# Plain MLP products of chunks 0 and 1 beside attention, Strassen blocks for chunks 2 and 3 only, split weights kept in DRAM

## The chip, the cores and the metric

The kernel runs on one core of one Trainium2 chip. The metric is the device time of one execution in microseconds. The kernel before takes 2695.92 us, the median of three runs (2693.48 to 2704.14). The profile is of one further execution of 2692.31 us, whose span in the trace is 2690.6 us.

## The reference

One layer over 2048 tokens of width 1024, all in float32:

```
h = rmsnorm(x);  q, k, v, u, vg = split(h @ w_in)                 # w_in 1024 x 2560
a = stick_breaking_attention(q, k, v)                             # 8 heads of 64, causal:
    # A[t,s] = sigmoid(z_ts) * prod_{s<j<t} (1 - sigmoid(z_tj)),  z = q.k / 8
b = gelu(u) * (W_s layernorm(gelu(vg)) + b_s)                     # 8 groups, 128x128 each
x = x + concat(rmsnorm(a), rmsnorm(b)) @ w_out                    # 1024 x 1024
x = x + square(relu(rmsnorm(x) @ w_up)) @ w_down                  # 1024 x 4096, 4096 x 1024
out = rmsnorm(x)
```

## The kernel before

The 2048 tokens are four chunks of 512. Every float32 product is made of three: each operand is split into a high part (a copy rounded by ScalarE, ACT, L79, or L82 with a gain) and a low part (the difference, VectorE, DVE, L80 or L83), and `mm3` (L85 to L89) issues high by high (L87), high by low (L88) and low by high (L89), each 128 x 128 against 128 x 512, into one PSUM tile. These are "products" below. A "set" is one operand tile of 4 x 128 x 512 with its two halves.

The stages in order:

- `proj` multiplies with w_in: chunks 0 and 1 in one pass, then chunk 2, then chunk 3. `weight` (L112) loads 512 KB tiles into `st` (3 buffers) and splits each into `w_in` (5 buffers), in each of the three passes: 20 tiles a pass.
- `attention` (L282 to L377) is a generator of short steps, 320 of them over the four chunks. One step issues two products for z (L311, L312, on the diagonal a mask L314 too), two sigmoids on ACT (L317, L319), a scan and a multiplication on DVE (L322 or L325, L323 or L326), then for an earlier step four transposes (L336) with the split of `aT` (L79 on ACT, L80 on DVE), and for one still earlier two products with v (L354, L355). L364 writes a head's output.
- `Out(c)` (L417 to L531) is the output projection of a chunk: `operands` transposes and splits, `weights` (L462) loads and splits w_out, `product` makes 192 products and adds to x (L489), `turn` norms and transposes into the MLP's right operand, kept in SBUF for chunks 0 and 1 and stored to `h_d` for 2 and 3.
- `up_plain` (L550 to L568) makes the first MLP product of chunks 0 and 1 plainly: 16 turns of 96 products. `keep_acts` (L542) forms four Strassen sums on GpSimd (POOL, L536 to L539) and stores seven matrices to `s_d` from POOL's queue (L544).
- `down_seven` (L663 to L780) makes the second product of two chunks by Strassen's seven block products: 8 groups of 168, 1344 in all. `sums_of_h` forms the sums of `h_d` on POOL, stored to `th_d`; `right_operands` (L585) loads and splits seven sets of them; `up_seven` (L595) does the first product of chunks 2 and 3 in seven blocks, 1344 products, and `down_seven` the second.

What orders the work: each engine runs its instructions in the order in which the Tile scheduler put them, and the DMAs that SP issues (`nc.sync`) start in SP's order, those of `nc.gpsimd` in POOL's. Pools of tiles decide when a buffer is free. `together(main, side, ratio)` (L784) takes one part of `main` up to its next yield and then `ratio` steps of `side`: attention is `side`, with R_A = 1.0 beside `proj`, R_O = 1.0 beside `Out` 0 and 1, R_U = 0.87 beside `up_plain`, which yields every 6 products. When attention has ended, these follow alone (L860 to L870): `Out` 2 and 3, `down_seven(0)` with `sums_of_h`, `right_operands`, `up_seven(1)`, `down_seven(1)`.

Of the kernel before, what the change touches and what calls it, by code (L numbers as in the profile page):

```python
# [8 lines left out]
F32 = mybir.dt.float32  # L9
# [7 lines left out]
P = 128  # L17
# [17 lines left out]
def block_kernel(ctx: ExitStack, tc: tile.TileContext, x, x_t, gmix, w_in, ln_g, ln_b, sgw, sgb,  # L35
# [30 lines left out]
    b_d = dram.tile([T, SBW], F32, name="b_d")  # L66

# [39 lines left out]
    def proj(cs, places, sp, gated_first):  # L107
# [170 lines left out]
    R_A, R_O, R_U = 1.0, 1.0, 0.87  # L278
# [107 lines left out]
    h_d = dram.tile([4, P, 2, 2, TC], F32, name="h_d")  # L386
    th_d = [dram.tile([P, 4, TC], F32, name=f"th_d{i}") for i in range(4)]
    s_d = [[dram.tile([7, P, 4, TC], F32, name=f"s_d{p}_{g}") for g in range(NG)] for p in range(2)]

    class Room:  # L390


        def __init__(self, pool, psum, bufs, big=None):
            self.pool, self.psum, self.bufs, self.big_pool = pool, psum, bufs, big or pool

        def big(self, shape, dtype=F32):
            return self.big_pool.tile([P] + list(shape), dtype, name="big", bufs=self.bufs["big"])

        def get(self, name, shape, dtype=F32):
            return self.pool.tile([P] + list(shape), dtype, name=name, bufs=self.bufs[name])  # L400

# [3 lines left out]
        def raw8(self, shape):  # L405
            return self.get("raw8", shape)

# [8 lines left out]

    class Out:  # L417


        def __init__(self, c, room, place):  # L420
            self.c, self.rm, self.place = c, room, place

        def operands(self):
            rm, c = self.rm, self.c
            bm = self.bm = rm.big([2, 4, TC], F32R)
            self.rbs = []
            for t2 in range(2):
# [492 lines left out]
```

## Time and profile before

| | |
|---|---|
| median of three runs | 2695.92 us |
| profiled execution; its span | 2692.31 us; 2690.6 us |
| PE busy; weight loads (PEld) | 2422.6 us (90%); 1955.5 us (73%) |
| DVE, ACT, POOL busy | 1936.3 us (72%); 1271.6 us (47%); 616.3 us (23%) |
| mean granted clock of TensorE | 0.955 |
| DMA queues of SP and of POOL, share of 16 engines' span | 44.7%; 2.9% |

By the trace's names the stages lie so: `proj` of chunks 0 and 1 from 0 to 265 us, of 2 and 3 with attention to 620, `Out` 0 and 1 with attention to 815, `up_plain` with attention to 1457 and alone to 1490, `Out` 2 and 3 to 1666, `down_seven(0)` to 2013, `right_operands` to 2042, `up_seven(1)` to 2350, `down_seven(1)` to the end. Matmuls are pipelined and their recorded lengths overlap, so PE's busy time is more than its work; how densely products follow each other is read from their number in a stretch. The clock is given as a share of full speed (1.0 is 2.4 GHz, 0.5 is 1.2 GHz).

### The profile page before, as it was taken

The page shows a single profiled execution, that of the slowest core. Times are in us where ns is not written, and L with a number is a line of the kernel's source. Part 1 is how long each engine was busy: PE and PEld are TensorE (multiplying, and loading weights), DVE is VectorE, ACT ScalarE, POOL GpSimd, SP SyncE. Part 2 cuts the span into 40 slices and gives each one's busy share as a digit, 9 for nine tenths or more (in the row PEclk, how much of TensorE's full clock was granted, in tenths as well). Part 3 has the DMA queues.
Part 4 walks back from the last instruction along what each step waited for, and adds up shares of the span by engine and source line. Part 5 has one row for each costly group of instructions (what it writes and reads, how often), then busy time and mean ns, then how long its engine had stood idle before and what let it go on. Part 6 is the DMA issues. An engine that isn't in the chain of part 4 may idle for free.

```text
span 2690.6 us, 30409 instructions
## 1 busy us (share of the span) xinstructions
PE 2422.6 (90%) x11136; PEld 1955.5 (73%) x11136; DVE 1936.3 (72%) x2424; ACT 1271.6 (47%) x2144; POOL 616.3 (23%) x395
## 2 busy tenths in 40 slices
PE   7999989898898989999999594799986999989997
PEld 5887777776677777777777483578875888778886
DVE  6634788878888878888894453577786666567777
ACT  6314556455646656665664432233344454433333
POOL 3100021101101121212122202543223232133331
PEclk9999999999999999999999797899997999999999
DMA  6347755457544454444441627554235444554422
GB/s 203 102 125 229 195 167 164 146 153 215 164 121 143 140 149 125 141 125 145 125 146 69 240 86 297 189 186 157 102 138 181 162 145 156 214 218 161 157 102 94
DMA packets 159941, 422.48 MB, mean 157 GB/s; under 512 B 12720, under 2 KB 29104, under 8 KB 151088
## 3 DMA queue, kind: packets, MB, share of 16 engines
q1 hardware_dynamic: 148064, 389.08, 44.7%
q0 software_dynamic: 7424, 29.36, 2.9%
q10 hardware_dynamic: 4304, 2.10, 0.3%
q8 instruction: 88, 1.44, 0.2%
q14 instruction: 61, 0.50, 0.1%
HBM read 303.05 MB, written 117.44 MB: 156 GB/s over the span
## 4 chain that ended last, share of the span: by engine, by line
PE 60%; DVE 20%; DMA 8%; ACT 4%; issue 4%; POOL 3%; SPq 1%; POOLq 0%; DVEq 0%; ACTq 0%
PE mm L88 17%; PE mm L89 17%; PE mm L87 17%; DVE w L80 4%; DVE pr L325 4%; PE tr L336 3%; DVE b L326 2%; PE av L354 2%; DVE aT L80 1%; PE av L355 1%; PE z L311 1%; PE z L312 1%; DMA raw<-h_d 1%; DMA raw<-s_d 1%; DVE pr L322 1%
## 5 line engine op out<-in xcount | busy, mean ns | idle before, releaser
L87 PE MATMUL mm<-big,w 128*128 128x512 f32 x960 | 380.0, 396 | 30.5 <-ACT w L79 29.6
L87 PE MATMUL mm<-w,w 128*128 128x512 f32 x896 | 349.7, 397 | 56.5 <-ACT w L79 56.5
L88 PE MATMUL mm<-big,w 128*128 128x512 f32 x960 | 378.8, 395 | 0.0
L89 PE MATMUL mm<-big,w 128*128 128x512 f32 x960 | 378.7, 394 | 0.1
L88 PE MATMUL mm<-w,w 128*128 128x512 f32 x896 | 359.5, 401 | 18.3 <-DVE w L80 16.5
L89 PE MATMUL mm<-w,w 128*128 128x512 f32 x896 | 355.9, 397 | 0.0
L80 DVE TENSOR_TENSOR w<-raw,w 128x1024 fp32r<-128x1024 f32 (+1 forms) x192 | 247.9, 1292 | 65.6 <-ACT w L79 65.0
L325 DVE TENSOR_TENSOR_SCAN pr<-kk,pr,zeros 128x513 f32<-128x513 f32 x192 | 259.8, 1353 | 40.1 <-ACT kk L317 37.0
L317 ACT ACTIVATE kk<-z 128x512 f32<-128x512 f32 (+2 forms) x320 | 171.0, 534 | 242.1 <-PE z L312 141.1
L79 ACT ACTIVATE w<-raw 128x1024 fp32r<-128x1024 f32 (+1 forms) x192 | 165.7, 871 | 185.7 <-PE mm L89 98.3
L336 PE MATMUL tr<-ident,b 128*128 128x128 f32 x1088 | 191.3, 284 | 61.5 <-DVE b L326 38.7
L79 ACT ACTIVATE w<-big 128x1024 fp32r<-128x1024 f32 x96 | 101.6, 1059 | 296.5 <-PE mm L89 199.6
L87 PEld LDWEIGHTS mm<-w,w 128*128 128x128 f32 x896 | 170.5, 192 | 97.0 <-ACT w L79 61.6
L87 PEld LDWEIGHTS mm<-big,w 128*128 128x128 f32 x960 | 182.5, 190 | 69.4 <-ACT w L79 30.2
L88 PEld LDWEIGHTS mm<-w,w 128*128 128x128 f32 x896 | 172.9, 193 | 63.8 <-DVE w L80 27.8
L80 DVE TENSOR_TENSOR w<-big,w 128x1024 fp32r<-128x1024 f32 x96 | 134.8, 1404 | 116.7 <-ACT w L79 116.7
L336 PEld LDWEIGHTS tr<-ident,b 128*128 128x128 f32 x1088 | 134.6, 145 | 105.9 <-DVE b L326 46.0
L89 PEld LDWEIGHTS mm<-big,w 128*128 128x128 f32 x960 | 182.3, 190 | 40.0 <-DVE w L80 0.8
L88 PEld LDWEIGHTS mm<-big,w 128*128 128x128 f32 x960 | 182.9, 190 | 37.4
L79 ACT ACTIVATE aT<-tr 128x512 fp32r<-128x512 f32 (+1 forms) x320 | 172.9, 542 | 67.3 <-PE tr L336 66.0
L80 DVE TENSOR_TENSOR aT<-tr,aT 128x512 fp32r<-128x512 f32 (+1 forms) x320 | 190.7, 596 | 13.8 <-ACT aT L79 13.5
L89 PEld LDWEIGHTS mm<-w,w 128*128 128x128 f32 x896 | 173.2, 193 | 36.0
(188 smaller groups left out, 5107.7 us busy)
## 6 DMA issues: line engine op xcount, KB each, us to landing
raw<-s_d SPq DMA_DIRECT2D x56, 1024.0 KB, 4.8
kt<-k_d SPq DMA_DIRECT2D x160, 256.0 KB, 4.7
big<-in_w_down SPq DMA_DIRECT2D x16, 2048.0 KB, 10.1
st<-in_w_in SPq DMA_DIRECT2D x60, 512.0 KB, 5.1
s_d<-acts POOLq DMA_DIRECT2D x16, 1792.0 KB, 7.7
s_d<-acts SPq DMA_DIRECT2D x16, 1792.0 KB, 6.2
vt<-v_d SPq DMA_DIRECT2D x80, 256.0 KB, 2.7
t<-in_w_out SPq DMA_DIRECT2D x32, 512.0 KB, 6.2
```

The source lines that it names most:

```text
L79: nc.scalar.activation(hi, src, AF.Copy)
L80: nc.vector.tensor_tensor(lo, src, hi.bitcast(F32), ALU.subtract)
L87: nc.tensor.matmul(ps, lh, rh, start=first, stop=False, skip_group_check=more)
L88: nc.tensor.matmul(ps, lh, rl, start=False, stop=False, skip_group_check=more)
L89: nc.tensor.matmul(ps, ll, rh, start=False, stop=last, skip_group_check=more)
L311: nc.tensor.matmul(z[:, :Z], ql, kt[:, 0, :Z], start=True, stop=False)
L312: nc.tensor.matmul(z[:, :Z], ql, kt[:, 1, :Z], start=False, stop=not diag)
L317: nc.scalar.activation(kk[:, :L], z[:, :L], AF.Sigmoid, scale=-QK_SCALE)
L325: nc.vector.tensor_tensor_scan(pr[:, ::-1], kk[:, ::-1], zeros, carry[tb], ALU.mult, ALU.add)
L326: nc.vector.tensor_tensor(b, b, pr[:, 1:TC + 1], ALU.mult)
L336: nc.tensor.transpose(tr[:, tb * P:(tb + 1) * P], bs[tb][:, j * P:(j + 1) * P], ident)
L354: nc.tensor.matmul(av[:, t0:], vt[:, j, :], aT[:, 0, t0:], start=first, stop=False)
```

## The change

- `weight` splits w_in once, in the pass of chunks 0 and 1, and stores each split tile (1 MB) to `wi_d` from POOL's queue (L123 of the changed kernel). The passes of chunks 2 and 3 load 1 MB from there straight into `w_in` on SP (L118), with no split.
- `Out(0)` stores its split w_out to `wo_d`, the other chunks load it. `product` yields every 6 products instead of 12, `turn` twice as often, and R_O is 0.5.
- One pool of 14 tiles of 8 KB a partition ("t8") holds all operands, inputs and sums of the stages beside attention, in turn.
- `up_plain` forms no Strassen sums and stores the activations themselves to `act_d` from SP; R_U is 0.49. `down_plain` replaces `down_seven(0)`: 8 groups of 192 products, 1536 instead of 1344.
- The order is now `up_plain`, `Out(2)` and `down_plain` beside attention; then, with attention done, `Out(3)` woven with the middle of `down_plain`, then the rest of `down_plain`, then alone `right_operands`, `up_seven`, `down_seven`.
- `right_operands` loads four sets from `h_d` and forms the differences on DVE between the splits; `sums_of_h` and `th_d` are gone. The gains of the norms are loaded once.

The diff, cut (what it removes stands in the functions above; the rest of `Out` changes only tiles and their shapes):

```diff
         def weight(col, k2):
+
+            w = sp.tile([P, 2, 2, 512], F32R, name="w_in", bufs=5)
+            if cs[0] > 0:
+                nc.sync.dma_start(w.bitcast(F32), wi_d[col, k2])
+                return w
             st = sp.tile([P, 2, 512], F32, name="st", bufs=3)
             nc.sync.dma_start(st, w_in[col, :, 2 * k2:2 * k2 + 2, :])
-            w = sp.tile([P, 2, 2, 512], F32R, name="w_in", bufs=5)
             split(w[:, 0], w[:, 1], st)
+            nc.gpsimd.dma_start(wi_d[col, k2], w.bitcast(F32))
             return w
 
...
 
-    R_A, R_O, R_U = 1.0, 1.0, 0.87
+    R_A, R_O, R_U = 1.0, 0.5, 0.49
+
...
     y_d = [dram.tile([P, NTB, D], F32, name=f"y_d{c}") for c in range(NC)]
-    h_d = dram.tile([4, P, 2, 2, TC], F32, name="h_d")
-    th_d = [dram.tile([P, 4, TC], F32, name=f"th_d{i}") for i in range(4)]
-    s_d = [[dram.tile([7, P, 4, TC], F32, name=f"s_d{p}_{g}") for g in range(NG)] for p in range(2)]
+    h_d = [[dram.tile([P, 4, TC], F32, name=f"h_d{i}_{kk}") for kk in range(2)] for i in range(2)]
+    act_d = [dram.tile([P, DFF // P, TC], F32, name=f"act_d{i}") for i in range(2)]
+    s_d = [dram.tile([7, P, 4, TC], F32, name=f"s_d{g}") for g in range(NG)]
...
+            return self.t8(shape, F32R), self.t8(shape, F32R)
+
...
+    def split4(hl, src):
+        for j in range(0, 4, 2):
+            split(hl[0][:, j:j + 2, :], hl[1][:, j:j + 2, :], src[:, j:j + 2, :])
+
...
+            if self.c > 0:
+                for i in range(2):
+                    nc.sync.dma_start(w[i].bitcast(F32), wo_d[half, part, i])
...
                     ts_ = slice(tb * P, (tb + 1) * P)
                     ps = rm.ps()
                     for e in range(4):
-                        mm3(ps, m[:, 0, e, ts_], m[:, 1, e, ts_], ws[e][0], ws[e][1], e == 0, e == 3)
+                        mm3(ps, m[0][:, e, ts_], m[1][:, e, ts_], ws[0][:, e, :], ws[1][:, e, :], e == 0, e == 3)
+                        if e == 1:
+                            yield
                     nc.vector.scalar_tensor_tensor(ys[tb][:, hs], ps, rr[tb], ys[tb][:, hs], ALU.mult, ALU.add)
...
+                    for i in range(2):
+                        nc.sync.dma_start(wo_d[half, part, i], ws[i].bitcast(F32))
 
             yield from group(0, 1, self.bm, self.rbs)
...
+    def keep_acts(q, acts):
+
+        a11, a12, a21, a22, s1, s2, s4 = (acts[:, i] for i in (0, 1, 6, 3, 4, 5, 2))
+        nc.vector.tensor_tensor(s1, a21, a22, ALU.add)
+        nc.vector.tensor_tensor(s2, s1, a11, ALU.subtract)
+        nc.vector.tensor_tensor(a21, a11, a21, ALU.subtract)
+        nc.vector.tensor_tensor(s4, a12, s2, ALU.subtract)
+        nc.sync.dma_start(s_d[q // 4][:, :, q % 4, :].rearrange("i p t -> p i t"), acts)
...
 
         for q in range(16):
-            acts = rm.get("acts", [7, TC])
+            acts = rm.t8([2, 2, TC])
+            st = rm.t8([2, 8, P])
...
+                            k == 0, k == KD - 1)
                         if k % 2 == 1 and k < KD - 1:
                             yield
...
+            for i in range(2):
+                nc.sync.dma_start(act_d[i][:, 2 * q:2 * q + 2, :], acts[:, i])
...
+            return a
+
+        def right(n, g):
+            st = rm.t8([4, 512])
+            nc.sync.dma_start(st, w_down[4 * g * P:4 * (g + 1) * P, n * 512:(n + 1) * 512]
+                              .rearrange("(f p) d -> p f d", p=P))
+            b = rm.pair([4, 512])
+            split4(b, st)
+            return b
+
+        ND = 8
+        c_now, n_now = 0, 0
+        for g in range(ND):
+            lefts, rights = {}, {}
+            for turn in range(4):
+                if turn == 2:
+                    c_now = 1 - c_now
+                elif turn > 0:
+                    n_now = 1 - n_now
+                c, n = c_now, n_now
+                if c not in lefts:
...
+                for tb in range(NTB):
+                    ts_ = slice(tb * P, (tb + 1) * P)
+                    ps = rm.ps()
+                    for k in range(4):
+                        mm3(ps, a[0][:, k, ts_], a[1][:, k, ts_], b[0][:, k, :], b[1][:, k, :], k == 0, k == 3)
+                        if k == 1:
+                            yield
+                    y = ys[4 * c + tb]
+                    nc.vector.tensor_tensor(y[:, ns], ps, y[:, ns], ALU.add)
+                    if g == ND - 1 and turn % 2 == 1:
+                        finish(rm, rm.t4([D], BF16), c, tb, y)
+                    yield
+
...
-        for i in ORDER:
-            st = rm.raw8([4, TC])
-            src = th_d[i - 3] if i >= 3 else h_d[:, :, (0, 1, 1)[i], (0, 0, 1)[i], :].rearrange("j p t -> p j t")
-            nc.sync.dma_start(st, src)
-            hc[i] = rm.big([2, 4, TC], F32R)
+        b = {}
+        for i, kk, name in ((0, 0, "raw8"), (1, 0, "raw8"), (1, 1, "acts"), (0, 1, "acts")):
...
+        def minus(dst, x, y):
             for j in range(0, 4, 2):
-                split(hc[i][:, 0, j:j + 2, :], hc[i][:, 1, j:j + 2, :], st[:, j:j + 2, :])
-            yield
...
+        def keep(i, src):
+            t = rm.big([2, 4, TC], F32R)
+            hc[i] = t
+            split4((t[:, 0], t[:, 1]), src)
+
+        keep(0, b11)
+        minus(b11, b12, b11)
+        keep(4, b11)
+        minus(b11, b22, b11)
+        keep(5, b11)
+        minus(b12, b22, b12)
+        keep(6, b12)
+        keep(1, b21)
+        minus(b21, b21, b11)
+        keep(3, b21)
+        keep(2, b22)
...
+        together(o.operands(), side, R_U)
+        together(o.product(), side, R_U)
+        together(o.turn(), side, R_U)
+        down = down_plain(rm)
+        assert together(down, side, R_U) is OPEN
+    with tc.tile_pool(name="ext", bufs=1, side="right", reuse_waits="tile") as ext, \
+            tc.tile_pool(name="ps_x2", bufs=5, space=PSUM, reuse_waits="tile") as ps_x2:
+        rm3 = Room(ext, ps_x2, dict(t8=8, t4=1))
+        o = Out(3, rm3)
+        for part in (o.operands, o.product, o.turn):
+            together(part(), down, 0.8)
+        together(down)
+    low.close()
     mm_stack.close()
-    with tc.tile_pool(name="ps_b", bufs=8, space=PSUM, reuse_waits="tile") as ps_b:
-        with tc.tile_pool(name="op2", bufs=1, reuse_waits="tile") as op2:
-            rm = Room(op2, ps_b, dict(big=4, w8=4, t4=10, ys=8, raw8=4))
-            o2, o3 = Out(2, rm, 0), Out(3, rm, 1)
-            together(o2.operands())
-            together(o3.operands())
-            together(o2.product())
-            turn = o2.turn()
-            together(o3.product(), turn, 0.25)
-            together(turn)
-            together(o3.turn())
-        with tc.tile_pool(name="mlp", bufs=1, reuse_waits="tile") as mlp:
-            rm = Room(mlp, ps_b, dict(big=7, w8=5, raw8=2, acts=2, t2=4))
-            main = down_seven(0, rm)
-            for _ in range(8):
-                next(main)
-            together(main, sums_of_h(rm), 0.25)
-            together(main)
-            hc = [None] * 7
-            together(right_operands(rm, hc))
-            together(up_seven(1, hc, rm))
-            together(down_seven(1, rm))
+    with tc.tile_pool(name="ps_b", bufs=8, space=PSUM, reuse_waits="tile") as ps_b, \
+            tc.tile_pool(name="mlp", bufs=1, reuse_waits="tile") as mlp:
+        rm = Room(mlp, ps_b, dict(big=7, w8=5, raw8=2, acts=2, t2=3))
+        hc = [None] * 7
+        right_operands(rm, hc)
+        together(up_seven(hc, rm))
+        together(down_seven(rm))
```

Two or three places show how the instructions move (names are the program's; in the changed kernel lines differ: L89 to L91 are the three products, L320 and L321 z, L345 the transposes, L363 and L364 av, L638 the sum into y, L82 the low part of a split).

PE beside attention in `up_plain`, in the kernel before. `mm` is a product of `up_plain`, z, tr and av are one step of attention:

```order
L336 MATMUL tr<-ident,b 128x128 x4
L354 MATMUL av<-aT,vt 128x512
L355 MATMUL av<-aT,vt 128x512
L87 MATMUL mm<-big,w_10410 128x512
L88 MATMUL mm<-big,w_10410 128x512
L89 MATMUL mm<-big,w_10410 128x512
L87 MATMUL mm<-big,w_10410 128x512
L88 MATMUL mm<-big,w_10410 128x512
L89 MATMUL mm<-big,w_10410 128x512
L311 MATMUL z<-kt,qt 128x256
L312 MATMUL z<-kt,qt 128x256
```

Here 6 products stand between two steps. In the changed kernel, at the same part of `up_plain`:

```order
L363 MATMUL av<-aT,vt 128x512
L364 MATMUL av<-aT,vt 128x512
L89 MATMUL mm<-t_6782,t_9205 128x512
L90 MATMUL mm<-t_6783,t_9205 128x512
L91 MATMUL mm<-t_6782,t_9206 128x512
L89 MATMUL mm<-t_6782,t_9205 128x512
L90 MATMUL mm<-t_6783,t_9205 128x512
L91 MATMUL mm<-t_6782,t_9206 128x512
...
L91 MATMUL mm<-t_5908,t_9488 128x512
L320 MATMUL z<-kt,qt 128x384
L321 MATMUL z<-kt,qt 128x384
```

What moved: the same step is now followed by 12 products, so the attention that stood beside `up_plain` alone reaches into `Out(2)` and `down_plain`.

DVE in the later part of the changed kernel's `down_plain`, with attention and `Out(3)` done. `t_12276` and `t_12278` are the sums y of one chunk, `t_12280` and `t_12282` those of the other, `mm` the product's PSUM tile, L82 the low part of a set for a later turn (`t_15341`, `t_15349`), in two pieces:

```order
L638 TENSOR_TENSOR t_12280<-mm,t_12280 128x512 x2
L638 TENSOR_TENSOR t_12282<-mm,t_12282 128x512
L82 TENSOR_TENSOR t_15341<-t_15338,t_15340 128x1024
L638 TENSOR_TENSOR t_12282<-mm,t_12282 128x512
L82 TENSOR_TENSOR t_15341<-t_15338,t_15340 128x1024
L638 TENSOR_TENSOR t_12276<-mm,t_12276 128x512 x2
L638 TENSOR_TENSOR t_12278<-mm,t_12278 128x512
L82 TENSOR_TENSOR t_15349<-t_15346,t_15348 128x1024
L638 TENSOR_TENSOR t_12278<-mm,t_12278 128x512
L82 TENSOR_TENSOR t_15349<-t_15346,t_15348 128x1024
L638 TENSOR_TENSOR t_12276<-mm,t_12276 128x512 x2
L638 TENSOR_TENSOR t_12278<-mm,t_12278 128x512
```

What moved: in place of the additions and Strassen forms of `down_seven(0)` there is one addition of 128x512 for each 12 products and eight pieces of split for each 192. A set is split in the turn before the one that uses it, and its second piece stands behind that turn's last addition.

SP at the end of the MLP of chunks 0 and 1, in the kernel before. `big` holds the finished outputs, `raw` are the tiles of `right_operands`, the last row the first weights of `up_seven`:

```order
L690 DMA out_y<-big 128x1024 x3
L589 DMA raw_16259<-th_d_92 128x2048
L690 DMA out_y<-big 128x1024
L589 DMA raw_16266<-th_d_93 128x2048
L690 DMA out_y<-big 128x1024 x4
L589 DMA raw_16273<-h_d 128x4x512
L589 DMA raw_16280<-th_d_90 128x2048
L589 DMA raw_16287<-h_d 128x4x512
L598 DMA raw_16294<-in_w_up 128x2x1024
```

And in the changed kernel (L648 stores the outputs, L654 loads `h_d`, L681 the weights of `up_seven`):

```order
L648 DMA out_y<-t_12276 128x1024 x2
L648 DMA out_y<-t_12278 128x1024 x2
L654 DMA raw_15932<-h_d_0_91 128x2048
L654 DMA raw_15934<-h_d_0_93 128x2048
L654 DMA acts<-h_d_1_94 128x2048
L654 DMA acts<-h_d_1_92 128x2048
L681 DMA raw_15983<-in_w_up 128x2x1024
```

What moved: the loads of the right operands stood among the output stores and stand behind all eight of them now; four 1 MB sets are loaded instead of seven.

## Rows read from the trace of the kernel before

**Rows 1.** The page: busy time by engine; PE by fortieths of the span, in tenths.

```profile
PE 2422.6 (90%) x11136; PEld 1955.5 (73%) x11136; DVE 1936.3 (72%) x2424; ACT 1271.6 (47%) x2144; POOL 616.3 (23%) x395
PE   7999989898898989999999594799986999989997
```

**Rows 2.** Windows by stage: length, busy PE, PEld, DVE, ACT, POOL (instructions), clock, DMA, GB/s.

```profile
265.00:620.00 355.00, 324.92 (x1618) 261.54 (x1618) 291.59 (x448) 197.04 (x386) 42.63 (x41) 0.98 0.58 167
...
1490.00:1666.00 176.00, 107.59 (x489) 87.99 (x489) 72.32 (x103) 57.47 (x100) 25.60 (x27) 0.80 0.58 216
1666.00:2013.00 347.00, 323.58 (x1344) 260.14 (x1344) 264.26 (x250) 119.14 (x125) 135.06 (x52) 0.95 0.43 156
2013.00:2042.00 29.00, 0.64 (x2) 0.44 (x2) 19.20 (x21) 13.62 (x17) 4.83 (x5) 0.59 0.70 254
...
815.00:2042.00 1227.00, 1059.42 (x4938) 854.58 (x4938) 899.85 (x1017) 582.41 (x1005) 304.57 (x174) 0.94 0.46 153
0.00:50.00 50.00, 40.57 (x156) 30.52 (x157) 31.04 (x52) 32.90 (x51) 13.41 (x24) 0.97 0.74 242
```

**Rows 3.** Windows: attention beside `proj`, beside `up_plain`, and `up_seven` alone.

```profile
500.00:600.00 100.00, 96.36 (x490) 78.68 (x489) 79.32 (x115) 53.48 (x101) 4.09 (x3) 1.00 0.55 156
2060.00:2340.00 280.00, 280.00 (x1237) 231.82 (x1236) 171.71 (x234) 142.37 (x235) 78.42 (x57) 1.00 0.43 155
1050.00:1150.00 100.00, 93.00 (x472) 74.86 (x471) 84.74 (x103) 61.55 (x121) 20.08 (x12) 1.00 0.47 144
```

**Rows 4.** PE's waits: line waited for, us in total, times, longest.

```profile
PE mm L87 <- ACT w L79: 86.1, 11, 33.0
PE tr L336 <- DVE b L326: 38.7, 23, 4.8
```

**Rows 5.** The chain that ended last, at 1640 us and in the norms at 2007: start, us, what.

```profile
1639.73 24.17 DMA raw<-s_d
...
2007.28 1.40 POOL nf_r L73
2008.71 1.28 DVE big L689
```

**Rows 6.** ACT by line: a split's high part; steps of attention from 815 us on.

```profile
L79 ACT ACTIVATE big<-raw 128x1024 fp32r<-128x1024 f32 x14 | 14.1, 1048 | 15.0 <-DMA raw<-h_d 8.4 <-issue 4.6 <-DMA raw<-th_d 1.9
L317 ACT ACTIVATE kk<-z x194: 262/597/648, 815.1 to 1436.2; 128x512 f32<-128x512 f32 x155, 128x128 f32<-128x128 f32 x13, 128x256 f32<-128x256 f32 x13, 128x384 f32<-128x384 f32 x13
```

**Rows 7.** PE's timeline around one full step beside `up_plain`: start, us, engine, line.

```profile
1202.66 0.40 PE L89 MATMUL mm<-big,w 128*128 128x512 f32 x1
1202.89 0.39 PE L311 MATMUL z<-kt,qt 128*128 128x512 f32 x1
...
1204.26 0.39 PE L87 MATMUL mm<-big,w 128*128 128x512 f32 x1
```

**Rows 8.** DVE by line and form: busy us, mean ns, idle before.

```profile
L325 DVE TENSOR_TENSOR_SCAN pr<-kk,pr,zeros 128x513 f32<-128x513 f32 x192 | 259.8, 1353 | 40.1 <-ACT kk L317 37.0
...
L80 DVE TENSOR_TENSOR aT<-tr,aT 128x512 fp32r<-128x512 f32 x224 | 152.0, 679 | 13.8 <-ACT aT L79 13.5
L326 DVE TENSOR_TENSOR b<-b,pr 128x512 f32<-128x512 f32 x192 | 148.7, 775 | 12.0
L678 DVE TENSOR_TENSOR big<-mm,big 128x512 f32<-128x512 f32 x208 | 139.6, 688 | 18.4 <-PE mm L89 18.4
...
L80 DVE TENSOR_TENSOR w_in<-st,w_in 128x1024 fp32r<-128x1024 f32 x60 | 74.8, 1253 | 17.3 <-ACT w_in L79 16.7
...
L80 DVE TENSOR_TENSOR big<-raw,big 128x1024 fp32r<-128x1024 f32 x14 | 16.6, 1218 | 8.1 <-ACT big L79 8.1
```

**Rows 9.** DMA issues: KB each, median us from issue to landing.

```profile
raw<-s_d SPq DMA_DIRECT2D x56, 1024.0 KB, 4.8
...
s_d<-acts POOLq DMA_DIRECT2D x16, 1792.0 KB, 7.7
s_d<-acts SPq DMA_DIRECT2D x16, 1792.0 KB, 6.2
```

More of the change, by code (lines that the diff above doesn't have):

```diff
@@ L66, in block_kernel @@
     b_d = dram.tile([T, SBW], F32, name="b_d")
+    wi_d = dram.tile([5, KD // 2, P, 2, 2, 512], F32, name="wi_d")
+    wo_d = dram.tile([2, 2, 2, P, 4, 512], F32, name="wo_d")
     def rsqrt_mean(pool, ssq, n, count, tag):
@@ L473, in weights @@
-            return ws
+            rm = self.rm
+            w = rm.pair([4, 512])
+            if self.c > 0:
+                for i in range(2):
+                    nc.sync.dma_start(w[i].bitcast(F32), wo_d[half, part, i])
+                return w
+            st = rm.t8([4, 512])
+            nc.sync.dma_start(st, w_out[part * 512:(part + 1) * 512, half * 512:(half + 1) * 512]
+                              .rearrange("(n p) d -> p n d", p=P))
+            for n in range(4):
+                split(w[0][:, n], w[1][:, n], st[:, n], outg_t[:, part * 4 + n:part * 4 + n + 1])
@@ L839, in block_kernel @@
         base.close()
-        with tc.tile_pool(name="hp", bufs=1, reuse_waits="tile") as hp:
-            hTs = []
-            with tc.tile_pool(name="op", bufs=1, reuse_waits="tile") as op:
-                rm = Room(op, ps_mm, dict(big=4, w8=3, t4=5, ys=5), hp)
-                for c in range(2):
-                    while steps[0] < 16 * (c + 1) * (c + 2) + NTB + LAG:
-                        next(side)
-                    o = Out(c, rm, None)
-                    together(o.operands(), side, R_O)
-                    together(o.product(), side, R_O)
-                    together(o.turn(), side, R_O)
-                    hTs.append(o.hT)
-            with tc.tile_pool(name="upp", bufs=1, reuse_waits="tile") as upp:
-                rm = Room(upp, ps_mm, dict(big=4, w8=4, t4=2, acts=2), hp)
-                main = up_plain(0, hTs, rm)
-                if together(main, side, R_U) is OPEN:
-                    together(main)
-                for _ in side:
-                    pass
@@ new lines, in block_kernel @@
+        gfin_t = gains.tile([P, D], F32, name="gfin_t")
+        low = ExitStack()
+        mp = low.enter_context(tc.tile_pool(name="mp", bufs=1, reuse_waits="tile"))
+        gmlp_t = mp.tile([P, D], F32, name="gmlp_t")
+        nc.sync.dma_start(gmlp_t, gmlp.broadcast_to([P, D]))
+        nc.sync.dma_start(gfin_t, gfin.broadcast_to([P, D]))
+        rm = Room(mp, ps_mm, dict(t8=N8, t4=2))
+        hTs = []
+        for c in range(2):
+            while steps[0] < 16 * (c + 1) * (c + 2) + NTB + LAG:
+                next(side)
+            o = Out(c, rm)
+            together(o.operands(), side, R_O)
+            together(o.product(), side, R_O)
+            together(o.turn(), side, R_O)
+            hTs.append(o.hT)
@@ new lines, in block_kernel @@
+        together(up_plain(hTs, rm), side, R_U)
+        while steps[0] < 16 * 3 * 4 + NTB + LAG:
+            next(side)
+        o = Out(2, rm)
+        together(o.operands(), side, R_U)
[10 more added lines that the diff above has]
+        together(down)
```

204 lines of the change are left out of this document (93 added, 111 removed).

## The prediction

> **What bounds the kernel now.** I read the page first. PE is busy 90% of the span, and its row by fortieths falls in three places only, the start, the stretch after the middle and once near 2030 us [rows 1]. So PE sets the time, and the question is where it stands still. The windows by stage answer it [rows 2]: beside attention (`proj` of chunks 2 and 3, 265 to 620 us) its weight loads fill 261.54 of 355 us; in the two output projections alone (1490 to 1666) 87.99 of 176 at a clock of 0.80; in `down_seven(0)` 260.14 of 347; and from 2013 to 2042 it does nothing. Against that stands `up_seven`, where 1237 products took 280 us without a pause, 0.2264 us each [rows 3]. In PE's waits the largest is for ACT's split of a loaded set, 86.1 us, one of 33.0; attention's own, for the multiplication on DVE, is 38.7 [rows 4]. The chain shows the 33 us as one burst, 24.17 us of loads from `s_d` [rows 5]. The start of the kernel and `proj` lie outside the change's large part.
>
> The Trainium skill (Perfetto Trace Analysis, § Identifying the Most-Contended Engine) holds PE's busy share for a poor measure and the share of weight loads for a good one. The dense stage agrees: 231.82 us of weight loads in 280 us of unbroken work, so a share of 0.83 is full. By PE's busy time the stretch from 815 to 2042 us would have only 1227 less 1059.42, or 168 us to give back; by its weight loads (854.58 / 0.83 = 1030) about 197 [rows 2, 3]. What follows goes by counted products.
>
> **What the change does, part by part.** All of it that is large lies between 815 and 2042 us of before, 1227 us [rows 2].
>
> *Work of PE in its place.* Products, by the loops: `up_plain` 1536, `Out` 2 and 3 192 each, `down_plain` 1536, in all 3456 (before: 3264, since `down_seven(0)` has 1344). From 815 us on 194 steps of attention remain, 155 of them 512 wide, 13 of these the last of a diagonal [rows 6]; so 142 full and 52 diagonal, and with those still in the pipe some 200. A full step costs PE the 1.37 us from 1202.89 to 1204.26 [rows 7]; a diagonal one I estimate at 1.0, its z, transposes and av being narrower. That is 142 x 1.37 + 58 x 1.0 = 253 us. A product beside attention takes 0.23 us (1202.66 to 1202.89) [rows 7]; I take 0.231. `up_plain` now gives a step every 6 / 0.49 = 12.2 products, so 125 steps; `Out(2)` yields 45 times, 22 steps; the other 54 stand in the first 660 products of `down_plain`. So 1536 + 192 + 660 = 2388 products at 0.231 (552 us) and 1068 dense ones at 0.2264 (242 us). The 96 transposes of `Out` 2 and 3 add some 8: a full step's 1.37 less four products leaves 0.45 for four of them, 0.11 each at most. Sum: 253 + 552 + 242 + 8 = 1055 us.
>
> *Losses that stay.* (a) `up_plain` beside attention. With 12 products a step `proj` kept 96.36 of 100 us, with about 7 `up_plain` kept 93.00 [rows 3]. The change makes 7 into 12, so I charge 3.6% of 510 us, 18 us; bounds 0 and 7% (36). (b) `down_plain` beside attention. Per step of 4.2 us (12.2 x 0.231 + 1.37) DVE has a scan 1.353, a multiplication 0.775, a split of aT 0.679, one addition 0.69 (the like of L678), and 0.6 for its share of eight pieces of split, 1.218 each, per 192 products [rows 8]: 4.1 of 4.2 us. It is nearly as full as PE. I charge 0.25 us a step, 13 us; bounds 0 and 1 us (54). (c) `Out(2)` beside attention: its first product waits for transposes, splits and a norm. `Out` 2 and 3 alone took 176 us for 384 products (87 us) and their transposes: some 40 us lost a chunk [rows 2]. Attention covers half, I take 20; bounds 5 and 40. (d) The dense rest of `down_plain` with `Out(3)`. A set's second piece stands behind the last addition of the turn before [the order of DVE]: addition 0.69 and split 1.22 make 1.9 us, against 1.6 us until the eighth product wants it. About 0.5 us for each of some 28 sets, 14 us. Bounds 0 and the price of `down_seven(0)`, whose 1344 products (304 us) took 347, 43 us for 56 sets, 0.75 a set (24 us for 32) [rows 2]. (e) The gap ahead of `up_seven`. SP has all eight output stores ahead of the loads of `h_d`, so the last norm (addition 0.69, square 1.05, power on POOL 1.40, scaling 1.28 and the handing over, some 5.5 us [rows 5, 6, 8]) comes first, then one 1 MB load (about 5) [rows 9], then 14 low parts and 8 differences on DVE at 1.218 [rows 8], 27 us, and a first weight: 39 us, where before the gap was 29 [rows 2]. Bounds 30 and 48; DVE orders it, ACT's 14 copies at 1.05 [rows 6] fit beside. Losses: 18 + 13 + 20 + 14 + 39 = 104.
>
> So the place of 1227 us takes 1055 + 104 = 1159, 68 us less.
>
> *What goes.* The burst of 24.17 us on `s_d` [rows 5] has no heir: the sets of `down_plain` are loaded one by one behind `up_plain`'s stores, and the products of `up_plain` to the end hide them at 4.8 us a set [rows 9]. What is late next is the split, counted in (d).
>
> *w_in and w_out in DRAM.* In chunks 2 and 3, 40 splits of 1.253 us leave DVE [rows 8], 50 us, and some 42 leave ACT. DVE is 0.79 busy there [rows 3], beside 3.6% idle of PE, so at best some 13 of the 355 us come back [rows 2]. Against it, a load goes straight into `w_in` and cannot start before PE has left that buffer; SP issues in order, and kt stands behind. I take 0, bounds -13 and +40 (a rival below). In the pass of chunks 0 and 1, 20 stores of 1 MB are added from POOL's queue. In the first 50 us DMA is 0.74 busy at 242 GB/s, with loads that PE waits for [rows 2]; the four stores that fall there are 4.2 MB, 17 us at that rate. Some of it finds room: I take 5, bounds 0 and 17. `wo_d` saves 12 sets of split beside attention and is within (c).
>
> *Unchanged.* `up_seven`, `down_seven` of chunks 2 and 3 and the end keep their instructions: 0, bounds -3 and +8, the latter if the gap's low clock [rows 2] lasts longer into `up_seven`.
>
> The sum: -68 + 5 = -63 us on a span of 2690.6, so 2627.6, a run of 2629.3. The profiled run was 3.6 us below the median of the runs shown (2692.31 against 2695.92); against the median the forecast is 2633.
>
> **Rivals.**
>
> *Sets come late (the other side).* All operands of `up_plain` and `down_plain` share one ring of 14 tiles. In `up_plain` the kept hT hold 8 of them and a turn takes four; in `down_plain` the sums y hold 4 and a set takes three. So one or two sets can be in flight. If the scheduler's order then leaves a load behind the last use of its tile, a set costs 4.8 us load, 2 x 1.05 and 2 x 1.22 of split, 9.3 us, less what 12 to 48 products (2.7 to 11 us) cover. There are 48 (16 turns of `up_plain`, 32 in `down_plain`). At 1.3 us each the 63 us are gone; at 2.2 us it is 106, and the time 2739. For it: 86.1 us of waits on just such splits [rows 4]. Against it: those 86 came in 11 waits, mostly the burst, and in the order of DVE the split of a set stands a turn ahead of its use.
>
> *w_in waits for PE.* With five buffers, one is free ahead. If each of the ten columns of chunks 2 and 3 loses 4 us to a load of 5 that cannot be early, +40: 2673. Against it: attention stands between the products, and before it was the same five buffers behind `st`.
>
> *POOL's stores hold the tiles.* Stores of `s_d` from POOL's queue landed in 7.7 us, the same from SP in 6.2 [rows 9]. A `w_in` tile is free only when its store has landed; 1.5 us for each of 20 is 30: 2663. Against it: that pass takes 265 us for 20 tiles, 13 us each. The Trainium skill (SBUF — State Buffer, § Who interferes with whom) says that a DMA issued by GpSimd can be starved by DVE; the 7.7 against 6.2 goes that way, though it may be other traffic.
>
> *Cleaner than thought.* Up at 1% (5), (b) 2, (c) 8, (d) 5, (e) 35, no price at the start: 55 instead of 109, 2579.
>
> **How the numbers follow.** Forecast 0.60; cleaner 0.16; w_in 0.10; POOL's stores 0.04; late sets 0.10, of which half end above before. Predicted 2633. Its own range is 2605 to 2660 (half the distance to the bounds of (a) to (e), which don't all fall on one side); the cleaner case and the waits of w_in carry it to 2578 and 2685. A measurement of this kernel tells 0.5% from no change, 13.5 us: faster is below 2682, slower above 2709. The forecast, the cleaner and POOL's case lie below 2682, and 0.06 of w_in's: with the late sets' 0.02, 0.88. Late sets give 0.05 slower and 0.02 faster; 0.07 remain between, 0.04 of w_in's and 0.03 of theirs.
>
> **What would show it.** Right: in the window of `up_plain` PE busy at 96% or more with the same steps reaching into `down_plain`; DVE above 0.9 there until attention ends; a gap of 35 to 45 us ahead of `up_seven`; no load burst over 10 us between 815 us and there; `proj` of chunks 2 and 3 within 355 +- 15 us. Wrong: waits of PE for ACT's splits of `t8` sets above 50 us in all (late sets), `z` or `mm` waits for `kt<-k_d` or `w_in<-wi_d` above 20 us in chunks 2 and 3, waits for `st` in the first 100 us above 15.

## The result and the profile after

The changed kernel takes 2620.86 us, the median of four runs (2617.47 to 2629.4), against 2694.73 us before (2693.48 to 2704.14). The ratio is 0.9723, 95% interval 0.9691 to 0.9755. Predicted were 2633 us, 2578 to 2685, faster at 0.88. The profiled run has a span of 2618.9 us, 71.7 less than before, where the sum had 63.

The page, busy time by engine and PE's fortieths, answers to [rows 1]:

```profile
PE 2445.8 (93%) x11328; PEld 1980.5 (76%) x11328; DVE 1720.0 (66%) x2296; ACT 1156.1 (44%) x2004; POOL 359.8 (14%) x287
PE   7899898998989999999989899999948999899997
```

192 products more, and PE's row now falls once only, near 1950 us. DVE lost 216 us of work. The windows by stage, columns as in [rows 2]; in the changed kernel the first three are `proj` with attention (to 640 us), `Out` 0 and 1 (to 834), `up_plain`, then `Out(2)`, `down_plain` with `Out(3)`, the gap, `up_seven`, `down_seven`:

```profile
640.00:834.00 194.00, 167.06 (x793) 131.04 (x794) 150.38 (x222) 100.14 (x199) 25.89 (x25) 0.91 0.66 227
...
834.00:1344.00 510.00, 507.30 (x2494) 417.55 (x2495) 329.69 (x420) 285.48 (x544) 12.93 (x14) 1.00 0.39 122
1344.00:1468.00 124.00, 104.95 (x495) 79.42 (x494) 91.68 (x122) 60.46 (x116) 9.51 (x9) 0.91 0.68 228
1468.00:1931.00 463.00, 459.67 (x2142) 379.20 (x2142) 290.68 (x376) 153.12 (x243) 14.62 (x19) 1.00 0.37 128
1931.00:1969.00 38.00, 0.44 (x2) 0.02 (x1) 27.72 (x26) 15.73 (x20) 3.69 (x4) 0.53 0.52 196
1969.00:2279.00 310.00, 307.90 (x1344) 254.16 (x1344) 188.76 (x255) 154.22 (x255) 87.47 (x63) 0.99 0.43 157
2279.00:2619.00 340.00, 311.79 (x1346) 253.23 (x1344) 255.83 (x260) 121.57 (x129) 109.52 (x40) 0.97 0.39 149
```

Read it by PE's weight loads: `up_plain` is at 0.82 and `down_plain` at 0.82 of the stretch, where 0.83 is full; `Out(2)` is at 0.64 and the gap at nothing. `up_seven` and `down_seven` are as before. What lay between 815 and 2042 us, 1227 us, now lies between 834 and 1969, 1135 us: 92 less, of which 19 are spent ahead of it, in the first 834 us.

PE's waits [rows 4]:

```profile
PE mm L89 <- ACT w L81: 49.1, 4, 37.7
PE tr L345 <- DVE aT L82: 20.7, 26, 3.0
PE tr L345 <- DVE b L332: 16.5, 22, 3.4
```

The waits for splits of loaded sets fell from 86.1 us in 11 to 49.1 in 4, and 37.7 of them are the gap. No wait for a set of `down_plain` or `up_plain` stands in the list.

Of the new rows of the DMA issues these two are loads; the transfers of attention stand between them:

```profile
w_in<-wi_d SPq DMA_DIRECT2D x40, 1024.0 KB, 7.6
kt<-k_d SPq DMA_DIRECT2D x160, 256.0 KB, 5.1
...
t<-wo_d SPq DMA_DIRECT2D x24, 1024.0 KB, 9.1
```

### The profile page after: what moved, and what is told of

Same layout as the page of the kernel before. It is cut to its first block, busy times and chain, and to the rows that moved or that the text cites. A ratio compares the mean times of both kernels' runs of the same rounds, so it can differ in the third digit from the quotient of the medians.

```text
span 2618.9 us, 30175 instructions
## 1 busy us (share of the span) xinstructions
PE 2445.8 (93%) x11328; PEld 1980.5 (76%) x11328; DVE 1720.0 (66%) x2296; ACT 1156.1 (44%) x2004; POOL 359.8 (14%) x287
## 4 chain that ended last, share of the span: by engine, by line
PE 74%; DVE 15%; DMA 4%; ACT 3%; issue 3%; POOL 1%; SPq 0%; POOLq 0%; DVEq 0%; ACTq 0%
PE mm L91 21%; PE mm L90 21%; PE mm L89 21%; PE tr L345 3%; DVE pr L334 2%; PE av L363 2%; PE av L364 2%; PE z L321 2%; PE z L320 2%; DVE pr L331 1%; DVE w L82 1%; DVE aT L82 1%; DVE t L82 1%; DVE b L335 1%; DMA w_in<-wi_d 1%
## 5 line engine op out<-in xcount | busy, mean ns | idle before, releaser
L91 PE MATMUL mm<-t,t 128*128 128x512 f32 x1280 | 501.0, 392 | 0.0
L90 PE MATMUL mm<-t,t 128*128 128x512 f32 x1280 | 500.5, 391 | 0.0
L89 PE MATMUL mm<-t,t 128*128 128x512 f32 x1280 | 498.1, 392 | 0.0
L334 DVE TENSOR_TENSOR_SCAN pr<-kk,pr,zeros 128x513 f32<-128x513 f32 x192 | 250.8, 1306 | 123.7 <-ACT kk L326 123.6
L326 ACT ACTIVATE kk<-z 128x512 f32<-128x512 f32 (+2 forms) x320 | 171.4, 536 | 325.8 <-PE z L321 214.3
L91 PEld LDWEIGHTS mm<-t,t 128*128 128x128 f32 x1280 | 240.6, 188 | 51.6
L89 PEld LDWEIGHTS mm<-t,t 128*128 128x128 f32 x1280 | 240.8, 188 | 50.7 <-ACT t L84 0.2
L90 PEld LDWEIGHTS mm<-t,t 128*128 128x128 f32 x1280 | 240.7, 188 | 50.5 <-DVE t L85 0.3
L345 PE MATMUL tr<-ident,b 128*128 128x128 f32 x1088 | 192.5, 286 | 45.8 <-DVE aT L82 20.7
L82 DVE TENSOR_TENSOR aT<-tr,aT 128x512 fp32r<-128x512 f32 (+1 forms) x320 | 190.6, 598 | 39.6 <-ACT aT L81 39.3
L89 PE MATMUL mm<-big,w 128*128 128x512 f32 x448 | 175.6, 392 | 37.7 <-ACT w L81 37.7
L345 PEld LDWEIGHTS tr<-ident,b 128*128 128x128 f32 x1088 | 134.7, 145 | 97.4 <-DVE aT L82 34.8
L89 PE MATMUL mm<-w,w 128*128 128x512 f32 x448 | 173.8, 393 | 11.6 <-ACT w L81 11.4
L90 PE MATMUL mm<-w,w 128*128 128x512 f32 x448 | 176.6, 394 | 6.8 <-DVE w L82 5.2
L91 PE MATMUL mm<-big,w 128*128 128x512 f32 x448 | 175.3, 392 | 2.0 <-DVE w L82 2.0
L90 PE MATMUL mm<-big,w 128*128 128x512 f32 x448 | 175.5, 392 | 0.0
L91 PE MATMUL mm<-w,w 128*128 128x512 f32 x448 | 175.2, 391 | 0.0
L81 ACT ACTIVATE t<-t 128x1024 fp32r<-128x1024 f32 x104 | 105.3, 1062 | 158.2 <-DMA t<-in_w_down 92.2
L328 ACT ACTIVATE b<-z 128x512 f32<-128x512 f32 (+2 forms) x320 | 171.1, 535 | 0.9 <-PE tr L345 0.9
L82 DVE TENSOR_TENSOR w<-raw,w 128x512 fp32r<-128x512 f32 (+1 forms) x136 | 157.3, 1158 | 15.4 <-ACT w L81 15.0
L363 PE MATMUL av<-aT,vt 128*128 128x512 f32 (+1 forms) x320 | 145.4, 455 | 13.8 <-DVE ao L373 9.5
```

The costliest lines, as they stand in the source:

```text
L81: nc.scalar.activation(hi, src, AF.Copy)
L82: nc.vector.tensor_tensor(lo, src, hi.bitcast(F32), ALU.subtract)
L89: nc.tensor.matmul(ps, lh, rh, start=first, stop=False, skip_group_check=more)
L90: nc.tensor.matmul(ps, lh, rl, start=False, stop=False, skip_group_check=more)
L91: nc.tensor.matmul(ps, ll, rh, start=False, stop=last, skip_group_check=more)
L326: nc.scalar.activation(kk[:, :L], z[:, :L], AF.Sigmoid, scale=-QK_SCALE)
```

## Experiments

The theory after the result: the gain is that `Out` 2 and 3 and the first `down` no longer stand alone with their loads, and the kept w_in is a loss. Each run's ratio is to the kernel before on the same chip. The line they are measured from is the changed kernel run again.

> The changed kernel itself, as the line to measure the edits from on the same chip. All theories: 2618 to 2624 us, ratio to before 0.972.

Measured 2625.9 us, ratio 0.9732 (0.9719 to 0.9746), 2 us above the range expected.

### The kept w_in

Without it, in both directions:

```diff
-            if cs[0] > 0:
-                nc.sync.dma_start(w.bitcast(F32), wi_d[col, k2])
-                return w
...
-            nc.gpsimd.dma_start(wi_d[col, k2], w.bitcast(F32))
```

> Only the keeping of split w_in is undone: no stores to wi_d, and chunks 2 and 3 load and split w_in again. Theory A (the stores crowd the first loads, and 1 MB loads into w_in come late in chunks 2 and 3): products of proj stand 6 us earlier from 60 us on and 15 us earlier at 600 us, as in the kernel before; time 15 us less than the changed kernel, 2606. Rival B (the 40 splits less on DVE pay, and the 15 us of lateness come from elsewhere, the order of attention): same or up to 13 us slower, 2621 to 2634.

Measured 2608.5, ratio 0.9669 (0.9655 to 0.9683), 17 us less than the changed kernel. Then the stores alone:

```diff
-            if cs[0] > 0:
-                nc.sync.dma_start(w.bitcast(F32), wi_d[col, k2])
-                return w
...
-            nc.gpsimd.dma_start(wi_d[col, k2], w.bitcast(F32))
+            if cs[0] == 0:
+                nc.gpsimd.dma_start(wi_d[col, k2], w.bitcast(F32))
```

> The 20 stores to wi_d stay, but chunks 2 and 3 load and split w_in again as in the kernel before; nothing reads wi_d. Theory A: the 6 us at the start stay, the 9 us of chunks 2 and 3 go, 2612. If the stores cost nothing by themselves: 2606, as with no stores at all. Rival B: 2621 to 2634, as the splits come back.

Measured 2616.72, ratio 0.9697 (0.9682 to 0.9713). So the stores cost some 8 us and the loads some 9, and theory A stands, the price of the stores being the weaker one (the intervals of these two runs just meet). By how much the high-by-high product of a given number, counted from 0, starts later than in the kernel before, in us, from the traces (64 at the start, 320 at the end of the first pass, 384 and 600 in chunks 2 and 3):

```
product                          64     320     384     600
changed kernel, run again        7.2    7.3    28.7    21.0
without the kept w_in            1.1    0.5    -1.2     0.4
stores only                      5.8    5.3     3.2     4.6
loads on GpSimd's queue          5.4    5.5    18.7    17.9
same, first column not kept      0.9    1.3    13.9    24.3
```

The start is late wherever the first stores stand, by 5 to 7 us. (The 28.7 is a product that stands right behind a bunch of attention; the product before it is 17.2 late.) Of what happens in chunks 2 and 3 the number of products between two z's in PE's records is the plainest view. Before, it is 12 almost throughout from the sixth number on. In the changed kernel it begins, after the first three, 30, 0, 0, 0, 68, 0, 1, 1, 26, 0, 0, 0, 64: attention comes four steps at a time, each waiting for DVE, with products alone in between. That the loads into `w_in` stand ahead of kt on SP was to be the reason:

```diff
-                nc.sync.dma_start(w.bitcast(F32), wi_d[col, k2])
+                nc.gpsimd.dma_start(w.bitcast(F32), wi_d[col, k2])
```

> The changed kernel with the 40 loads of split w_in issued from GpSimd's queue in place of SP's; the stores to wi_d stay. Theory A (on SP the loads of kt stand behind loads into w_in that wait for PE, so attention comes in bunches): steps stand 12 products apart again, chunks 2 and 3 lose their 9 us and may gain up to 13 from DVE's fewer splits, 2604 to 2617; the 7 us at the start stay. Rival B (the traffic of 1 MB loads is what is late): 2624 to 2630.

Measured 2631.93, ratio 0.9757 (0.9735 to 0.9778): above both ranges and no gain, so theory A is wrong as to the price. The bunches went (12, 12, 12, 12, 12, 6, 18, 12 ...), and another wait took their place. The waits of PE and of POOL in this run, from 230 to 660 us:

```profile
PE mm L89 <- DMA w_in<-wi_d: 15.8, 14, 2.6
PE z L320 <- DMA qt<-q_d: 8.5, 1, 8.5
...
POOL w_in L118 <- PE mm L91: 168.7, 26, 36.1
```

The queue that issues the loads stands 168.7 us for PE to leave a `w_in` buffer, and PE then waits 14 times for what was loaded into it; on SP (the changed kernel run again) PE waited 5.6 us for `w_in`, but SP stood 17.9 us at those loads in nine waits for PE, with kt queued behind. A load straight into one of five buffers, four of which are in use, can't be early on either queue. The first column kept out:

```diff
-            if cs[0] > 0:
+            if cs[0] > 0 and col != 4:
...
-            nc.gpsimd.dma_start(wi_d[col, k2], w.bitcast(F32))
+            if cs[0] == 0 and col != 4:
+                nc.gpsimd.dma_start(wi_d[col, k2], w.bitcast(F32))
```

> As the one before, and the first column of w_in (4 of 20 tiles, those split in the first 50 us) is neither stored nor loaded back, but split again in chunks 2 and 3. Theory A (four stores crowd the first loads): the 7 us at the start go too, 2597 to 2610. Rival B (the start is late by the later stores): as the run before it, within 3 us, or slower for the 8 splits that come back.

Measured 2632.09, ratio 0.9768 (0.9744 to 0.9793). Half right: the start is on time (0.9 us late at product 64), so the four first stores are what crowds it: in the first 100 us ACT waits 22.4 us for the loads of `st` in the changed kernel run again, 14.1 in the kernel before and 14.7 here. But the time stays, as chunks 2 and 3 end later than in the run before it (24.3 at product 600); PE waited 18.2 us for `w_in<-wi_d` there. Why they end later is open.

The relief on DVE bought no time on the whole: from 230 to 660 us its work is 281.70 us in the changed kernel and 341.14 without the kept w_in, with PE's weight loads the other way round:

```profile
230.00:660.00 430.00, 387.15 (x1862) 304.53 (x1861) 281.70 (x461) 191.73 (x404) 50.95 (x55) 0.97 0.76 228
```

```profile
230.00:660.00 430.00, 390.73 (x1906) 312.42 (x1905) 341.14 (x522) 241.14 (x463) 56.00 (x58) 0.96 0.64 186
```

(the changed kernel run again, and the one without the kept w_in). This does not show that DVE's work there is free. In the same stretch PE's listed waits for DVE come to 32.2 us without the kept w_in, 30.3 in the changed kernel run again, and 20.6 and 17.6 in the two runs with the loads on GpSimd's queue, where attention comes evenly; its waits for DMA go 3.9, 8.5, 27.0 and 26.1. So PE did wait less for DVE where the order let it, and the loads took more than that back. No run has the relief without the loads.

### Why `up_plain` is dense

```diff
...
-        together(up_plain(hTs, rm), side, R_U)
+        beside(up_plain(hTs, rm), 0.87)
...
```

(`beside` goes on alone when attention has ended; `Out(2)` and `down_plain` then have no attention beside them.)

> The changed kernel with 0.87 in place of 0.49 steps a yield beside up_plain, so about 7 products stand between two steps, as before the change; attention ends within up_plain, and the output projection of chunk 2 and all of the second product stand alone. Theory A (12 products between steps make up_plain dense): PE loses some 7% where steps stand, 35 us, and time is 15 to 45 us over the changed kernel, 2640 to 2670. Rival B (the four sums on GpSimd, gone with the change, were what thinned it): under 2% lost, 2616 to 2636.

```diff
+        spare = rm.t4([2, TC])
...
+            nc.gpsimd.tensor_tensor(spare[:, 0], acts[:, 0, 0], acts[:, 0, 1], ALU.add)
+            nc.gpsimd.tensor_tensor(spare[:, 1], spare[:, 0], acts[:, 1, 0], ALU.subtract)
+            nc.gpsimd.tensor_tensor(spare[:, 0], acts[:, 0, 0], acts[:, 1, 1], ALU.subtract)
+            nc.gpsimd.tensor_tensor(spare[:, 1], acts[:, 0, 1], spare[:, 1], ALU.subtract)
```

> The changed kernel with four sums of 128x512 on GpSimd for each of the 16 turns of up_plain, as before the change, written to a spare tile that nothing reads. Theory A (spacing): up_plain stays dense, 0 to 5 us more, 2626 to 2631. Rival B (the sums slow DVE's scans, and PE waits): 3 to 7% of 510 us, 2641 to 2661.

Measured 2636.79 (0.9773, 0.9753 to 0.9793), 11 us over the changed kernel, and 2628.98 (0.9744, 0.9724 to 0.9764), not told apart from it. The windows inside `up_plain`, in this order: the kernel before, seven products a step without sums, twelve with sums, twelve without (the changed kernel run again):

```profile
850.00:1350.00 500.00, 463.89 (x2322) 373.91 (x2321) 423.80 (x505) 301.05 (x596) 107.45 (x67) 0.98 0.45 135
```

```profile
850.00:1350.00 500.00, 487.58 (x2486) 394.17 (x2484) 420.01 (x543) 324.60 (x640) 13.00 (x12) 1.00 0.43 127
```

```profile
850.00:1340.00 490.00, 486.06 (x2390) 399.33 (x2389) 337.92 (x396) 272.81 (x519) 102.14 (x70) 1.00 0.40 121
```

```profile
850.00:1340.00 490.00, 487.35 (x2407) 401.13 (x2405) 314.34 (x400) 275.48 (x526) 9.99 (x11) 1.00 0.40 122
```

PE idles 7.2%, 2.5%, 0.8% and 0.5%. Neither theory holds alone: either edit takes away most of the 7%, which stands only where two things come together, a DVE at 0.84 and sums that lengthen its work. The row of the multiplication in attention shows the latter, at twelve products a step with the sums and without:

```profile
L335 DVE TENSOR_TENSOR b<-b,pr 128x512 f32<-128x512 f32 x83 | 73.2, 882 | 6.8
```

```profile
L335 DVE TENSOR_TENSOR b<-b,pr 128x512 f32<-128x512 f32 x83 | 57.3, 690 | 7.2 <-ACT t L453 0.5
```

At seven products a step the multiplication takes 0.787 us in the kernel before and 0.689 without the sums, and the scan 1.372 and 1.284.

The run with seven products a step says something more. In it attention ends at 1417 us, within `up_plain`, as in the kernel before, and both projections and `down_plain` stand without it. Yet it is only 11 us over the changed kernel, about what the 2 points of idle time more cost in these 500 us, and 61 under the kernel before. So that fewer steps stand in `up_plain` and attention reaches further is worth about 11 of the 72 us, and its company brought `Out(2)` no gain that shows. Without it `Out(2)` stands from 1464 to 1535 us, 71 us with one wait of 10 for `t<-wo_d`, its norms between products of `down_plain`; with it that stretch is 124 us, of which 28 steps of attention are some 35.

### What standing alone costs

```diff
-            together(part(), down, 0.8)
+            together(part())
```

> The changed kernel with the output projection of chunk 3 run alone after attention, in place of woven with the middle of down_plain. Theory A (a projection alone loses some 40 us to its loads, transposes and norms, as in the kernel before, and weaving hides them): 30 to 45 us more than the changed kernel, 2656 to 2671. Rival B (the loads are early anyway, and down_plain's own waits move): within 10 us, 2616 to 2636.

Measured 2623.68, ratio 0.9727 (0.9713 to 0.974): nothing. But the edit didn't do what it was for. In PE's order 365 products stand between the transposes of `Out(3)`'s operands and those of its `turn`, and only 192 are its own: the scheduler filled in 173 of `down_plain` by itself, as in the changed kernel, ratio or no ratio. So it says nothing on standing alone. The next takes the filling away:

```diff
+        together(down)
         rm3 = Room(ext, ps_x2, dict(t8=8, t4=1))
...
-            together(part(), down, 0.8)
-        together(down)
+            together(part())
```

> The changed kernel with the output projection of chunk 3 after the whole of down_plain, so that no products of down_plain can fill its waits; in the run before, the scheduler had still put some 170 of them in between. Theory A (a projection alone loses some 40 us, and 5 to 15 more for storing and loading its result right ahead of up_seven): 2656 to 2680. Rival B (the loss before the change was the burst on s_d and the low clock alone): within 15 us of the changed kernel, up to 2641.

Measured 2677.55, ratio 0.9921 (0.9893 to 0.9949): 52 us over the changed kernel. Theory A stands. `Out(3)` is now the stretch from 1882 to 1989 us, with the gap behind it, and PE's waits there:

```profile
1882.00:1989.00 107.00, 63.00 (x233) 48.90 (x232) 24.89 (x35) 14.47 (x23) 7.33 (x8) 0.75 0.33 129
```

```profile
PE mm L89 <- ACT w L81: 34.8, 1, 34.8
PE mm L89 <- DMA t<-wo_d: 30.4, 4, 16.2
PE mm L542 <- DVE t L537: 11.9, 3, 4.0
```

107 us for 192 products, 43 us of work at 0.2264 each: the rest is its loads, 30.4 us, its norms, 11.9, its transposes, and a clock of 0.75 in the mean. The burst on `s_d` of the kernel before has no part in this loss, as the run loads nothing from `s_d` there. What replacing the first `down` by plain products is worth by itself no run shows.

### The gap, and two versions together

```diff
...
+                if q == 0:
+                    next(rights)
                 if len(slots) % 2 == 0:
                     operand.pair = rm.w8([2, 2, 512])
...
-        right_operands(rm, hc)
-        together(up_seven(hc, rm))
+        together(up_seven(hc, rm, right_operands(rm, hc)))
```

(`right_operands` yields after each set; the weights of the first turn are loaded into a tile of another ring.)

> The sets of the right operands are formed one by one, each just ahead of the split weight that meets it in the first of up_seven's 16 turns; the work is the same. Theory A (the 37.7 us gap is DVE's 22 pieces in a row, and products need only the first set): PE starts about 22 us earlier, waits again for later sets, and 10 to 15 us remain as a gain, 2606 to 2611. Rival B (DVE's whole chain, 27 us of pieces and 4 of weights, sets the end of the first turn whatever the order): within 3 us of the changed kernel.

Measured 2620.08, ratio 0.9715 (0.9701 to 0.9729), 6 us less, between the theories, and by the intervals, which meet, hardly told apart from none. PE's waits around the gap:

```profile
PE mm L89 <- ACT big L81: 22.7, 3, 20.4
PE mm L89 <- ACT w L81: 5.7, 2, 2.9
PE mm L90 <- DVE big L82: 2.1, 2, 1.6
```

The gap itself fell from 37.7 to 20.4 us; PE waited again for some later sets and weights, 10 us in all, and ran at a clock of 0.77 in the 34 us behind it. The window of those 34 us:

```profile
1956.00:1990.00 34.00, 23.77 (x77) 17.38 (x77) 33.50 (x32) 19.39 (x26) 8.50 (x4) 0.77 0.21 73
```

DVE is busy 33.50 of 34 us, so its chain is the bound that remains.

The two gains together, the second with `Out(2)` splitting plain w_out:

> The two edits that gained, together: no split w_in in DRAM (17 us less by itself) and the right operands formed one by one ahead of up_seven's first turn (5 to 6 us less by itself). If they are independent, as theory A has it (one lies before 620 us, one after 1930): 22 us under the changed kernel, 2600 to 2606 beside 2626. Rival B (an earlier stage gives back in a later one): 2609 or more.

```diff
-            if self.c > 0:
+            if self.c in (1, 3):
```

> As the run before it, and the output projection of chunk 2 loads w_out plain (4 MB) and splits it, in place of 8 MB of split halves. Theory A (the burst of 30 MB around this projection, with loads landing in 14 us, sets the 36 us lost there): 5 to 15 us less than the run before it. Rival B (the order of attention's steps there, which stays the same, sets the loss): within 3 us of it.

Measured 2602.28 (0.9651, 0.9638 to 0.9665) and 2598.16 (0.9634, 0.9621 to 0.9647). The first is 24 us under the changed kernel (22 by the ratios), where the two gains by themselves add up to 23: they are independent. The second's 4 us are not settled (the intervals meet); half the load did not free `Out(2)`, where the order has attention stand nine steps in a row and then 126 products alone in both. The last version is the fastest seen, 3.7% under the kernel before.

## Why the prediction was right

The sign and the size came out, by terms that were off both ways: the stretches that came out shorter than predicted gave 52 us, those that came out longer took 43, and that the sum was within 9 us is in part luck. From the text of the sum, each stretch as predicted (work and loss) and as measured:

| | predicted | measured |
|---|---|---|
| start and `proj`, `Out` 0, 1 | +5 | +19 |
| `up_plain` (a) | 513 + 18 | 510 |
| `Out(2)` (c) | 76 + 20 | 124 |
| `down_plain`, `Out(3)` (b, d) | 466 + 27 | 463 |
| gap (e) | 39 | 38 |
| `up_seven`, `down_seven` | 0 | +1 |

- *Work.* Right in sum, not stretch by stretch. By ACT's first sigmoids (L326) 122, 28 and 43 steps stand in the three stretches, where 125, 22 and 54 were counted. At the prediction's own prices a step and a product that is 509, 84 and 452 us of work, 1045 in place of 1055; the losses below are what is left over, estimates by some us.
- *(a), mis-sized, 18 against about 3.* The 3.6% was read off a stretch of `proj`, where DVE is 0.79 busy [rows 3]; in `up_plain` of the changed kernel run again it is 0.64. With twelve products a step and no sums on GpSimd, 0.5% is lost.
- *(b), mis-sized, with (d) 27 against about 11.* DVE was to be 98% busy beside attention; from 1468 to 1668 us of the changed kernel it was 167.16 of 200 us, and its scan and multiplication there were:

```profile
1468.00:1668.00 200.00, 198.14 (x954) 162.82 (x954) 167.16 (x214) 93.67 (x161) 1.69 (x2) 1.00 0.38 120
```

```profile
L334 DVE TENSOR_TENSOR_SCAN pr<-kk,pr,zeros 128x513 f32<-128x513 f32 x35 | 44.8, 1280 | 8.9 <-ACT kk L326 8.9
...
L335 DVE TENSOR_TENSOR b<-b,pr 128x512 f32<-128x512 f32 x35 | 24.0, 686 | 1.8
```

  The prediction took 1.353 and 0.775, from rows that GpSimd's sums had lengthened [rows 8], and every step at full width.
- *(d), mis-sized, its 14 within those 27.* A second piece behind the last addition did not stop PE: from 1668 to 1931 us the one wait listed is 1.5 us for a norm. The order of DVE showed what could be late, not that PE would wait for it.
- *(c), mis-sized, 20 against about 40.* The 76 is the prediction's 22 steps, 192 products and transposes; 28 steps stood there, some 8 us more, the rest is loss. The loads came in a burst here, by the DMA issues from 1340 to 1480 us of the changed kernel:

```profile
t<-wo_d SPq DMA_DIRECT2D x8, 1024.0 KB, 14.2
kt<-k_d SPq DMA_DIRECT2D x16, 256.0 KB, 11.2
```

  But PE's waits from 1340 to 1470 us are for attention's own steps, 9.7 us for their split on DVE and 0.8 for a load:

```profile
PE tr L345 <- DVE aT L82: 9.7, 12, 2.7
...
PE z L320 <- DMA kt<-k_d: 0.8, 1, 0.8
```

  Where nine steps stand in a row, DVE is busy without a break and PE is not:

```profile
1350.00:1360.00 10.00, 6.09 (x30) 3.84 (x29) 10.00 (x13) 9.95 (x17) 1.14 (x1) 1.00 0.56 180
1360.00:1370.00 10.00, 6.79 (x29) 4.66 (x28) 9.90 (x10) 5.29 (x12) 3.50 (x2) 0.66 1.03 421
```

  With half the load winning as little, the order in bunches is the better explanation; no run took it away.
- *(e).* Right in size and cause: DVE's pieces in a row. That undoing the order wins no more than 6 us was not foreseen.
- *The burst.* Right that no wait of PE takes its place. But a burst of loads over 10 us, which the prediction named as a thing that would not come, did: from 1360 to 1390 us the DMA engines are full, at 311 to 421 GB/s. Its other sign that failed is DVE above 0.9 until attention ends (0.65 in `up_plain`, 0.84 behind it). The experiments give the price of the whole idea: some 50 us for one projection with nothing beside it.
- *Kept w_in, mis-sized, +5 against some 17.* The start was right: 5 to 7 us, by the four first stores. For chunks 2 and 3 the value taken was 0; the rival named the wait (a load that can't begin before PE leaves its buffer, kt behind it on SP) at 40 us, and it came at a quarter of that. Its 50 us less on DVE came to no gain: PE does wait for DVE in those chunks, but where it waited less the loads took more back.
- *Late sets, POOL's stores.* The first did not come; of the second only the crowding at the start.

## What to carry to other kernels

Ask of every stage that stands alone what it would cost beside independent products, and measure the cost by taking the products away: here one projection of 43 us of work took 107 alone. Which products they are mattered less here: with attention ended early, a few of `down_plain` and the other projection's were nearly enough. Keeping a result in DRAM to save work on DVE adds a load that can start only when its buffer is free; here the loads cost more than the saved work gave. A loss read off another stage comes with that stage's own neighbours; the row to use is one with the same ones.

## What the runs showed of the hardware

A DVE multiplication of two 128x512 operands took 0.690 us without sums on GpSimd and, beside sums that kept GpSimd busy a fifth of the time, 0.787 in the mean in the kernel before and 0.882 in the run with the sums put back. The Trainium skill (SBUF — State Buffer, § Who interferes with whom) has a DVE instruction with two SBUF inputs contend with a GpSimd instruction that reads SBUF, which these rows agree with. A 1 MB load took 4.8 us at the median among the loads of `s_d` [rows 9] and 14.2 where 32 MB moved in 140 us.
